# Conditioning columns of an encoder kernel, summed by VectorE from transposed weights

## The chip, the cores and the metric

The kernel runs on one core of a Trainium2 chip. The metric is the device time of one execution in microseconds, as the median of several runs; lower is better. Five engines work side by side, each through its own list of instructions in order: TensorE (PE; its weight loads are listed apart as PEld), VectorE (DVE), ScalarE (ACT), GpSimd (POOL) and SyncE (SP), which here issues nearly all transfers. They wait for one another by semaphores.

## The reference, cut to what matters

Two encoder layers over 512 tokens of width 1024, one with neighbourhood attention and one with Fourier mixing, each followed by a gated FFN. In every layer six vectors (shift, scale and gate of two sub-layers) come from one conditioning vector c:

```
cs = silu(c)                                     # 1024 values
mod = cs @ ada_w[i] + ada_b[i]                   # (1024) @ (1024 x 6144)
sh1, sc1, g1, sh2, sc2, g2 = split(mod, 6)
u = x * (1 + sc1) + sh1
x = layer_norm(ALPHA * x + (1 + g1) * mixer(u))
u = x * (1 + sc2) + sh2
x = layer_norm(ALPHA * x + (1 + g2) * conv_ffn(u))
```

All is float32. `ada_w` is 2 x 1024 x 6144, 50 MB, and is read once.

## The kernel before, in words

Activations lie transposed, features on the 128 partitions in eight chunks of 128 and tokens along the row. To keep float32 precision each operand is split into a rounded high half and the rest (`hi`, `lo`; `u0h`, `u0l`), and a product becomes three matmuls: high by high, high by low, low by high (`mm3`). ScalarE makes the high half (L232), VectorE the low one (L233).

A shift or a scale is needed as columns: feature k*128+p on partition p, column k. A gate is needed as a row. Both are summed in the same way: the weights come with the 1024 inputs on the partitions in eight tiles, VectorE scales each tile by its column of `cs` and adds it into an accumulator `acc` (L127, L129), and TensorE sums the accumulator over the partitions by a product with ones. This ends in one of three ways:

- First stage (`cond_first`, `cond_accumulate`, `cond_reduce`, `cond_finish`): for each chunk k of the input 256 columns of weights, shift and scale of that chunk, are accumulated (L400; the first steps on ScalarE, L398), reduced by four fp32 matmuls into the bank `red` (eight records in the trace), and finished by two small VectorE operations (L412, L413). Then ScalarE computes the input (L424, L425), VectorE its low half (L426), and TensorE runs 9 products of 512 columns for Q and K (`first_qk`) and 12 for V (`first_v`). Chunk 0 goes by `cond_first`, partly by fp32 matmuls of the raw weights with `cs`.
- `sum_cols`: for the FFN of layer 0, sixteen 1-column fp32 products (`sc`, `sh`), slipped between the triple products of the output projection `wo`.
- `ada_cols`: for the four other vectors of this kind, four 512-column products each with ones, and then VectorE takes the diagonal out of two banks. They stand in the up and down projections of the FFN of layer 0 (`steps_up0`, `steps_dn0`).

Tiles come from pools: `wraw` (4 buffers for raw weights), `big` (31 buffers of 4 KB a partition), `wsp`. A transfer is issued when its buffer is free, in the order of SyncE's list. GpSimd adds the attention bias tables (`bx`) and a mask, both loaded behind the first stage's weights, for the score maxima (L585), and scales the probabilities (L599). A scheduler orders each engine's list, except inside `tc.manual_schedule`, where it stays as written; `after` holds back what stands in it until an instruction is issued. The attention loop from its second pair on is already in written order.

Of the kernel before, what the change touches and what calls it, by code (L numbers as in the profile page):

```python
# [49 lines left out]

@with_exitstack
def tile_hybrid_encoder(ctx: ExitStack, tc: tile.TileContext, xT, x, cols_d, rows_d, ada0, ada_w, wqk0, wqk, wv,
# [5 lines left out]
    big = ctx.enter_context(tc.tile_pool(name="big", bufs=31))  # L58
# [24 lines left out]
    between = []  # L83

    def mm3(o, lh, ll, rh, rl, start, stop):
        mm(o, lh, rh, start, False)
        mm(o, lh, rl, False, False)
        mm(o, ll, rh, False, stop)
        if between:
            product, k = between.pop(0)  # L90
            product(k)
# [25 lines left out]


    def ada_accumulate(l, v, result):

        acc = None
        for k in range(KT):
            raw = wraw.tile([P, D], F32, tag="raw", name=f"ada_{l}_{v}_{k}")
            nc.sync.dma_start(out=raw, in_=ada_w[l, k * P : (k + 1) * P, v * D : (v + 1) * D])
# [24 lines left out]

    def ada_cols(accs, l, v, name):  # L150

        bs = ada_row_sums(accs[(l, v)], name)
        col = sml.tile([P, KT], F32, tag="adacol", name=f"{name}_col")
        for h in range(2):
            t = tmp.tile([P, 4, P], F32, tag="t", name=f"{name}_d{h}")
            V.tensor_tensor(out=t, in0=bs[h].rearrange("p (k q) -> p k q", q=P),
                            in1=ident.unsqueeze(1).to_broadcast([P, 4, P]), op=ALU.mult)
            V.tensor_reduce(out=col[:, 4 * h : 4 * h + 4], in_=t, axis=mybir.AxisListType.X, op=ALU.add)
        V.tensor_tensor(out=col, in0=col, in1=adab(l, v), op=ALU.add)
        return col  # L160

    def sum_cols(acc, name):

        b = bank(name)

        def product(k):
            mm(b[:, k : k + 1], acc[:, k * P : (k + 1) * P], f32(ones_r[:, 0:1]), True, True)

        between.extend((product, k) for k in range(KT))
        return b  # L170

    def biased(b, l, v, name):
        assert not between
        col = sml.tile([P, KT], F32, tag="adacol", name=f"{name}_col")
        V.tensor_tensor(out=col, in0=b[:, 0:KT], in1=adab(l, v), op=ALU.add)
        return col
# [174 lines left out]
    def load_chunk(k):  # L351

        raws = []
        n = 2 if k == 0 else 4
        for h in range(2):
            raw = bigt([P, 4, 256], F32, f"ada0_{k}_{h}")
            for i in range(0, 4, n):
                nc.sync.dma_start(out=raw[:, i : i + n, :], in_=ada0[k, :, 4 * h + i : 4 * h + i + n, :])
            raws.append(raw)
# [12 lines left out]
    accq, redq, done = {}, {}, {}  # L372

    def cond_first():

        acc, red = tmp.tile([P, 256], F32, tag="t", name="acc00"), bank("red", aux=True)
        for i in range(KT):
            r = raws[0][i // 4][:, i % 4, :]
            if i < 4:
                for b in range(2):  # L380
                    mm(red[:, b : b + 1], r[:, b * P : (b + 1) * P], cs[:, i : i + 1], i == 0 and b == 0, False)
            elif i == 4:
                V.tensor_scalar(out=acc, in0=r, scalar1=cs[:, i : i + 1], scalar2=None, op0=ALU.mult)
            else:
                V.scalar_tensor_tensor(out=acc, in0=r, scalar=cs[:, i : i + 1], in1=acc, op0=ALU.mult, op1=ALU.add)
        for b in range(2):
            mm(red[:, b : b + 1], acc[:, b * P : (b + 1) * P], f32(ones_r[:, 0:1]), False, b == 1)
        redq[0] = red

    def cond_accumulate(k):  # L390

        pair = tmp.tile([P, 2, 256], F32, tag="t", name="acc0")
        for i in range(KT):
            r, o = raws[k][i // 4][:, i % 4, :], pair[:, i % 2, :]
            if i < 2 and k == 1:
                V.tensor_scalar(out=o, in0=r, scalar1=cs[:, i : i + 1], scalar2=None, op0=ALU.mult)
            elif i < 2:
                A.mul(o, r, cs[:, i : i + 1])  # L398
            else:
                V.scalar_tensor_tensor(out=o, in0=r, scalar=cs[:, i : i + 1], in1=o, op0=ALU.mult, op1=ALU.add)  # L400
        accq[k] = pair

    def cond_reduce(k):
        pair, red = accq.pop(k), bank("red", aux=True)
        for b in range(2):
            for j in range(2):
                mm(red[:, b : b + 1], pair[:, j, b * P : (b + 1) * P], f32(ones_r[:, 0:1]), j == 0, j == 1)
        redq[k] = red

    def cond_finish(k):  # L410
        red = redq.pop(k)
        V.tensor_tensor(out=mod0[:, KT + k : KT + k + 1], in0=red[:, 0:1], in1=adab(0, 0)[:, k : k + 1], op=ALU.add)  # L412
        done["mod"] = V.scalar_tensor_tensor(out=mod0[:, k : k + 1], in0=red[:, 1:2], scalar=1.0,  # L413
                                             in1=adab(0, 1)[:, k : k + 1], op0=ALU.add, op1=ALU.add)
        x_ = xt[k // 2][:, k % 2, :]
        uh, ul = u0[0][k // 2][:, k % 2, :], u0[1][k // 2][:, k % 2, :]
        scale, bias = mod0[:, k : k + 1], mod0[:, KT + k : KT + k + 1]
        if k == 0:
            t = tmp.tile([P, S], F32, tag="t", name="u00")
            done["act"] = A.activation(out=uh, in_=x_, func=AF.Identity, scale=scale, bias=bias)  # L420
            V.tensor_scalar(out=t, in0=x_, scalar1=scale, scalar2=bias, op0=ALU.mult, op1=ALU.add)
            x_ = t
        else:
            A.activation(out=x_, in_=x_, func=AF.Identity, scale=scale, bias=bias)  # L424
            done["act"] = A.copy(out=uh, in_=x_)  # L425
        return V.tensor_tensor(out=ul, in0=x_, in1=f32(uh), op=ALU.subtract)  # L426
# [16 lines left out]
    cond_first()  # L443
    W.emit(iqk0[0])
    with after(cond_finish(0)):
        cond_accumulate(1)
    with after(done["act"]):
        W.emit(iv0[0])
    for k in range(KT):
        if k + 3 < KT:  # L450
            raws.append(load_chunk(k + 3))
        first_qk(k)
        if k + 1 < KT:
            cond_reduce(k + 1)
            cond_finish(k + 1)
        if k % 2 == 0 and k + 2 < KT:
            with after(done["act"]):
                W.emit(iv0[k // 2 + 1])
        if k + 2 < KT:
            with after(done["mod"]):  # L460
                cond_accumulate(k + 2)
        first_v(k)
# [189 lines left out]
    ada_list = [(0, 2), (0, 4), (0, 3), (0, 5), (1, 1), (1, 0), (1, 2), (1, 4), (1, 3), (1, 5)]  # L652

    def ada_iter():
        for l, v in ada_list:
            yield from ada_accumulate(l, v, accs)
# [173 lines left out]
    sc = sum_cols(accs[(0, 4)], "sc2_0")  # L830
    sh = sum_cols(accs[(0, 3)], "sh2_0")
# [4 lines left out]
    m1 = modulation(biased(sh, 0, 3, "sh2_0"), biased(sc, 0, 4, "sc2_0"), (0, 0), "ffn0")  # L836
# [15 lines left out]
    def steps_up0(f):  # L852
# [4 lines left out]
        if f == 12:  # L857
# [273 lines left out]
```

## Time and profile before

| | |
|---|---|
| median of 3 runs | 1066.25 us (1064.4 to 1066.55) |
| the profiled execution | 1064.35 us, span 1062.6 us |
| TensorE busy | 1045.4 us, 98% of the span |
| VectorE, ScalarE, GpSimd busy | 73%, 41%, 9% |
| transfers | 157.24 MB, mean 148 GB/s |

The span is the time from the first to the last instruction of the profiled execution. A matmul's record covers its latency, and records overlap: what a matmul costs is read from the distance of the starts, not from its duration.

### The profile page before, as it was taken

How to read it: one execution, taken by the hardware profiler on the slowest of the kernel's cores; microseconds unless marked ns; L12 is line 12 of the kernel's file. 1: busy time of each engine (PE TensorE's matmuls, PEld its weight loads, DVE VectorE, ACT ScalarE, POOL GpSimd, SP SyncE). 2: the span in 40 equal slices, each digit the busy share in tenths (PEclk: the TensorE clock that was granted, in tenths of full speed). 3: DMA queues.
4: the chain of work that ended last, by engine and by line, in shares of the span. 5: the costliest groups of instructions: out<-in, count | busy, mean ns of one | idle time of the engine just before them, and what ended most of it. 6: DMA issues, size and time to landing. Idle time of an engine off the chain costs nothing.

```text
span 1062.6 us, 13633 instructions
## 1 busy us (share of the span) xinstructions
PE 1045.4 (98%) x5140; PEld 875.8 (82%) x5140; DVE 771.0 (73%) x1227; ACT 433.6 (41%) x738; POOL 98.6 (9%) x136
## 2 busy tenths in 40 slices
PE   7999999999999999999999999999999999999996
PEld 6878888888988888888888788898888888888885
DVE  6779898867789888886654879868876666532366
ACT  4445566545544444444132135454344444422300
POOL 0133565600000000000000000000000000000000
PEclk9999999999999999999999999999999999999998
DMA  9877454550355756553885005313454333243301
GB/s 351 289 243 238 131 158 135 183 164 11 105 176 177 231 190 192 178 179 105 294 279 178 1 1 171 107 54 125 129 169 134 104 99 100 79 160 99 119 20 60
DMA packets 46290, 157.24 MB, mean 148 GB/s; under 512 B 5136, under 2 KB 7696, under 8 KB 46224
## 3 DMA queue, kind: packets, MB, share of 16 engines
q1 hardware_dynamic: 46080, 156.24, 44.3%
q8 instruction: 40, 0.66, 0.3%
q14 instruction: 26, 0.21, 0.1%
q10 hardware_dynamic: 144, 0.13, 0.0%
HBM read 154.25 MB, written 2.10 MB: 147 GB/s over the span
## 4 chain that ended last, share of the span: by engine, by line
PE 91%; DVE 3%; DMA 2%; POOL 2%; issue 1%; SPq 0%; ACT 0%; DVEq 0%; POOLq 0%; ACTq 0%
PE up L81 45%; PE dn L81 23%; PE wo L81 4%; PE qk L81 4%; PE fo L81 4%; PE v L81 2%; POOL p L599 1%; PE q L81 1%; PE av L634 1%; PE fy L81 1%; PE pt L620 1%; PE s L81 1%; PE tr L307 1%; PE red L81 1%; DMA bx<-in_rpb_dram 1%
## 5 line engine op out<-in xcount | busy, mean ns | idle before, releaser
L233 DVE TENSOR_TENSOR lo<-raw,hi 128x1024 fp32r<-128x1024 f32 (+1 forms) x173 | 209.8, 1221 | 126.4 <-ACT hi L232 125.9
L232 ACT CAST hi<-raw 128x1024 fp32r<-128x1024 f32 (+1 forms) x173 | 179.0, 1044 | 245.0 <-PE up L81 128.7
L81 PE MATMUL dn<-hi,h 128*128 128x512 f32 (+1 forms) x720 | 218.2, 384 | 0.0
L81 PEld LDWEIGHTS dn<-hi,h 128*128 128x128 f32 x720 | 134.2, 188 | 27.0
L81 PE MATMUL up<-u1l,hi 128*128 128x512 f32 (+1 forms) x384 | 142.7, 372 | 0.0
L81 PE MATMUL up<-u3h,hi 128*128 128x512 f32 (+1 forms) x384 | 142.8, 372 | 0.0
L81 PE MATMUL up<-u1h,lo 128*128 128x512 f32 (+1 forms) x384 | 142.7, 372 | 0.0
L81 PE MATMUL up<-u1h,hi 128*128 128x512 f32 (+1 forms) x384 | 142.6, 372 | 0.0
L81 PE MATMUL up<-u3l,hi 128*128 128x512 f32 (+1 forms) x384 | 142.6, 371 | 0.0
L81 PE MATMUL up<-u3h,lo 128*128 128x512 f32 (+1 forms) x384 | 142.6, 371 | 0.0
L81 PE MATMUL dn<-lo,h 128*128 128x512 f32 (+1 forms) x360 | 138.4, 384 | 0.0
L129 DVE SCALAR_TENSOR_TENSOR acc<-ada,cs,acc 128x1024 f32<-128x1024 f32 x70 | 92.4, 1321 | 11.3 <-DMA ada<-in_ada_w_dram 11.1
L267 POOL TENSOR_TENSOR y<-ve,mhalf 128x1 f32<-128x1 f32 x16 | 10.8, 672 | 833.6 <-DVE ve L265 833.6
L81 PEld LDWEIGHTS up<-u1l,hi 128*128 128x128 f32 x384 | 72.3, 188 | 12.6 <-DVE u1l L317 0.2
L81 PEld LDWEIGHTS up<-u3h,hi 128*128 128x128 f32 x384 | 72.3, 188 | 12.6
L81 PEld LDWEIGHTS up<-u1h,lo 128*128 128x128 f32 x384 | 72.3, 188 | 12.5
L81 PEld LDWEIGHTS up<-u1h,hi 128*128 128x128 f32 x384 | 72.2, 188 | 12.6
L81 PEld LDWEIGHTS up<-u3h,lo 128*128 128x128 f32 x384 | 72.3, 188 | 12.5
L81 PEld LDWEIGHTS up<-u3l,hi 128*128 128x128 f32 x384 | 72.3, 188 | 12.4
L81 PEld LDWEIGHTS dn<-lo,h 128*128 128x128 f32 x360 | 67.6, 188 | 13.5
L599 POOL TENSOR_SCALAR p<-p,rs 128x256 f32<-128x256 f32 x64 | 58.1, 926 | 63.7 <-DVE rs L597 63.5
L747 ACT ACTIVATE gel<-conv 128x512 f32<-128x512 f32 x44 | 27.8, 632 | 63.9 <-DVE conv L744 63.5
(220 smaller groups left out, 1600.8 us busy)
## 6 DMA issues: line engine op xcount, KB each, us to landing
raw<-in_up_dram SPq DMA_DIRECT2D x88, 512.0 KB, 3.6
ada<-in_ada_w_dram SPq DMA_DIRECT2D x80, 512.0 KB, 4.8
raw<-in_down_dram SPq DMA_DIRECT2D x44, 512.0 KB, 4.7
ada<-in_ada_dram SPq DMA_DIRECT2D x14, 512.0 KB, 10.8
raw<-in_wqk_dram SPq DMA_DIRECT2D x13, 512.0 KB, 5.0
raw<-in_wv_dram SPq DMA_DIRECT2D x8, 512.0 KB, 6.5
raw<-in_wo_dram SPq DMA_DIRECT2D x8, 512.0 KB, 3.5
raw<-in_fnwo_dram SPq DMA_DIRECT2D x8, 512.0 KB, 4.5
```

The source lines that it names most:

```text
L81: return T.matmul(o, lhsT=lhsT, rhs=rhs, start=start, stop=stop)
L129: V.scalar_tensor_tensor(out=acc, in0=raw, scalar=cs[:, k : k + 1], in1=acc, op0=ALU.mult, op1=ALU.add)
L232: A.copy(out=hi, in_=raw)
L233: eng.tensor_tensor(out=lo, in0=raw, in1=f32(hi), op=ALU.subtract)
L267: power = G.tensor_tensor(out=y, in0=ve, in1=mhalf, op=ALU.pow)
L307: T.transpose(out=b[:, j * P : (j + 1) * P], in_=X[s][:, k * P : (k + 1) * P], identity=ident)
L599: norm = G.tensor_scalar(out=pt[:, j, :], in0=pt[:, j, :], scalar1=rs[:, j : j + 1], scalar2=0.0, op0=ALU.mult, op1=ALU.add)
L620: T.transpose(out=o, in_=pt[:, j, f : f + P], identity=ident)
L634: T.matmul(b[:, o : o + e - a], lhsT=v, rhs=z[:, a:e][:, ::-1], start=n == 0 and m == 0, stop=n == 3 and m == 1, skip_group_check=True)
L747: A.activation(out=q, in_=t, func=AF.Square)
```

## The change

The weights of the shifts and scales lie transposed in memory: outputs on the partitions, inputs along the row. silu(c) is laid out once along a row and on all partitions (`cs_row`): eight fp32 matmuls of a `cs` column, broadcast, with the identity, into two banks, and two ScalarE copies. A VectorE instruction multiplies 1024 weights of a partition by `cs_row`, sums them, starts from the bias and writes one element of a column; its output goes over the raw weights. So eight such instructions make a whole column tile without TensorE. The gates stay as they were. The functions `cond_*`, `sum_cols`, `ada_cols` and `biased` go. The bytes and the order of the first stage's transfers stay. The first stage is written in issue order for VectorE, ScalarE and TensorE, and the pool `big` has 30 buffers.

```diff
-    big = ctx.enter_context(tc.tile_pool(name="big", bufs=31))
+    big = ctx.enter_context(tc.tile_pool(name="big", bufs=30))
...
+    cs_row = const.tile([P, D], F32, name="cs_row")
+
+    def fill_cs_row():
+        b = [bank(f"csb{h}", aux=True) for h in range(2)]
+        for k in range(KT):
+            mm(b[k // 4][:, k % 4 * P : (k % 4 + 1) * P], cs[:, k : k + 1].to_broadcast([P, P]), ident, True, True)
+        for h in range(2):
+            A.copy(out=cs_row[:, h * 512 : (h + 1) * 512], in_=b[h])
+
+
+    def weigh_rows(raw, c, col, start):
+
+        return V.tensor_tensor_reduce(out=raw, in0=raw, in1=cs_row[:, c], op0=ALU.mult, op1=ALU.add, scale=1.0,
+                                      scalar=start, accum_out=col)
+
+    def ada_columns(l, v, result):
+
+        for k in range(KT):
+            raw = wraw.tile([P, D], F32, tag="raw", name=f"ada_{l}_{v}_{k}")
+            nc.sync.dma_start(out=raw, in_=ada_w[ADA[(l, v)], k])
+            if k == 0:
+                col = const.tile([P, KT], F32, name=f"col_{l}_{v}")
+            weigh_rows(raw, slice(0, D), col[:, k : k + 1], adab(l, v)[:, k : k + 1])
+            if k == KT - 1:
+                result[(l, v)] = col
+            yield
...
+    def cond(k):
+
+        for b, start in enumerate((adab(0, 0), ada01)):
+            o = mod0[:, (1 - b) * KT + k : (1 - b) * KT + k + 1]
+            start = start[:, k : k + 1]
+            if k == 0:
+                half = sml.tile([P, 1], F32, tag="t0", name="half")
+                weigh_rows(raws[k][b][:, 0:512], slice(0, 512), half, start)
+                done["mod"] = weigh_rows(raws[k][b][:, 512:D], slice(512, D), o, half)
             else:
...
+                done["mod"] = weigh_rows(raws[k][b], slice(0, D), o, start)
...
-        for n, (w, u) in enumerate(((wh, uh), (wh, ul), (wl, uh))):
+        for n, (w, u) in enumerate(((wh, uh), (wl, uh), (wh, ul))):
...
+    with tc.manual_schedule(engines={mybir.EngineType.DVE, mybir.EngineType.Activation, mybir.EngineType.PE}):
+        fill_cs_row()
+        cond(0)
+        first_input(0)
         W.emit(iv0[0])
...
+        cond(1)
+        for k in range(KT):
+            if k + 3 < KT:
+                raws.append(load_chunk(k + 3))
+            first_qk(k)
+            W.emit(iv0[k // 2] if k % 2 == 0 else iqk0[k // 2 + 1] if k + 1 < KT else iqk[1][1])
+            if k + 1 < KT:
+                first_input(k + 1)
+            if k + 2 < KT:
+                cond(k + 2)
+            first_v(k)
...
-    sc = sum_cols(accs[(0, 4)], "sc2_0")
-    sh = sum_cols(accs[(0, 3)], "sh2_0")
...
-    m1 = modulation(biased(sh, 0, 3, "sh2_0"), biased(sc, 0, 4, "sc2_0"), (0, 0), "ffn0")
+    m1 = modulation(accs[(0, 3)], accs[(0, 4)], (0, 0), "ffn0")
...
-        if f == 12:
-            fst["sc"] = ada_cols(accs, 1, 1, "sc1_1")
...
-            m = modulation(ada_cols(accs, 1, 0, "sh1_1"), fst["sc"], (0, 1), "fn")
+            m = modulation(accs[(1, 0)], accs[(1, 1)], (0, 1), "fn")
...
-        if f == 4:
-            fst["sc"] = ada_cols(accs, 1, 4, "sc2_1")
         if f == 8:
-            fst["m3"] = modulation(ada_cols(accs, 1, 3, "sh2_1"), fst["sc"], (1, 0), "ffn1")
+            fst["m3"] = modulation(accs[(1, 3)], accs[(1, 4)], (1, 0), "ffn1")
```

On TensorE the program begins so before, up to the first product with the low weights (`q`, `k`: banks of the first two heads; `u0h`, `u0l`: the halves of the input's first chunk pair):

```order
L81 MATMUL red<-cs,ada_0_0_112 128x1 x8
L81 MATMUL red<-ones_r,acc_139 128x1 x2
L81 MATMUL q_109<-u0h_96,hi_155 128x512
L81 MATMUL k_110<-u0h_96,hi_155 128x512
L81 MATMUL q_111<-u0h_96,hi_155 128x512
```

and so after the change:

```order
L84 MATMUL csb_144<-ident,cs 128x128 x4
L84 MATMUL csb_145<-ident,cs 128x128 x4
L84 MATMUL q_110<-u0h_97,hi_164 128x512
L84 MATMUL k_111<-u0h_97,hi_164 128x512
L84 MATMUL q_112<-u0h_97,hi_164 128x512
```

The products with the raw weights make room for the eight that lay out silu(c), which need no weights.

Between the Q and K products of a chunk and its V products (`v_0` to `v_3`: four token blocks), in the middle of the first stage, TensorE has this before:

```order
L81 MATMUL q_109<-u0h_98,lo_304 128x512
L81 MATMUL k_110<-u0h_98,lo_304 128x512
L81 MATMUL q_111<-u0h_98,lo_304 128x512
L81 MATMUL red<-ones_r,acc_413 128x1 x4
L81 MATMUL v_0_105<-hi_307,u0h_98 128x512
L81 MATMUL v_1_106<-hi_307,u0h_98 128x512
```

and this after:

```order
L84 MATMUL q_110<-u0l_103,hi_299 128x512
L84 MATMUL k_111<-u0l_103,hi_299 128x512
L84 MATMUL q_112<-u0l_103,hi_299 128x512
L84 MATMUL v_0_106<-hi_333,u0h_99 128x512
L84 MATMUL v_1_107<-hi_333,u0h_99 128x512
```

The four `red` matmuls are gone, and the products with the low input stand last instead of in the middle.

VectorE has, for one to two chunks of the first stage, before:

```order
L400 SCALAR_TENSOR_TENSOR acc_259<-ada_3_0_178,cs,acc_259 128x256 x2
L400 SCALAR_TENSOR_TENSOR acc_259<-ada_3_1_180,cs,acc_259 128x256 x4
L426 TENSOR_TENSOR u0l_101<-xt_133,u0h_97 128x512
L412 TENSOR_TENSOR mod_104<-red,cols 128x1
L413 SCALAR_TENSOR_TENSOR mod_104<-red,cols 128x1
L400 SCALAR_TENSOR_TENSOR acc_311<-ada_4_0_230,cs,acc_311 128x256 x2
L400 SCALAR_TENSOR_TENSOR acc_311<-ada_4_1_232,cs,acc_311 128x256 x2
```

and after (the rows named ISA are the sums, with the read of the accumulator behind each):

```order
L397 TENSOR_TENSOR u0l_102<-xt_136,u0h_98 128x512
L128 ISA ada_3_0_176,mod_105<-ada_3_0_176,cs_row,cols 128x1024
L128 ISA mod_105 128x1
L128 ISA ada_3_1_178,mod_105<-ada_3_1_178,cs_row,ada_113 128x1024
L128 ISA mod_105 128x1
L229 TENSOR_TENSOR lo_260<-raw_140,hi_259 128x1024
L397 TENSOR_TENSOR u0l_102<-xt_136,u0h_98 128x512
```

The small operations behind `red` are gone, two sums of 1024 elements stand in place of six accumulations of 256, and the split of the next weights stands where VectorE waits for ScalarE's input.

## Rows read from the trace of the kernel before

**Rows 1.** The page: busy time of the engines; the chain's shares by engine.

```profile
PE 1045.4 (98%) x5140; PEld 875.8 (82%) x5140; DVE 771.0 (73%) x1227; ACT 433.6 (41%) x738; POOL 98.6 (9%) x136
...
PE 91%; DVE 3%; DMA 2%; POOL 2%; issue 1%; SPq 0%; ACT 0%; DVEq 0%; POOLq 0%; ACTq 0%
```

**Rows 2.** By stretch: PE, PEld, DVE, ACT, POOL busy, clock, DMA share, GB/s.

```profile
0.00:40.00 40.00, 32.75 (x151) 27.26 (x151) 25.76 (x61) 17.52 (x27) 0.87 (x8) 1.00 0.96 366
40.00:60.00 20.00, 19.75 (x96) 16.08 (x95) 15.14 (x29) 11.45 (x17) 4.14 (x6) 1.00 0.56 171
```

**Rows 3.** Timeline to 17 us: start, duration, engine, what [idle before, releaser].

```profile
3.79 0.17 DVE L116 TENSOR_TENSOR cs<-cs,cols 128x8 f32<-128x8 f32 x1
...
4.96 3.49 PEld L81 LDWEIGHTS red<-cs,ada 128*128 128x128 f32 x16 [4.96 <-DVE cs L116]
...
9.18 0.83 ACT L232 CAST hi<-raw 128x768 fp32r<-128x768 f32 x1 [5.86 <-DMA raw<-in_wqk_dram]
...
10.34 0.81 ACT L420 ACTIVATE u0h<-xt,mod 128x512 fp32r<-128x512 f32 x1 [0.33 <-DVE mod L413]
...
11.21 0.79 PE L81 MATMUL q<-u0h,hi 128*128 128x512 f32 x1 [1.16 <-ACT u0h L420]
...
14.36 0.63 PE L81 MATMUL k<-u0h,lo 128*128 128x512 f32 x1
...
14.79 0.63 PE L81 MATMUL q<-u0h,lo 128*128 128x512 f32 x1
...
16.38 1.18 PE L81 MATMUL v<-hi,u0h 128*128 128x512 f32 x4
```

**Rows 4.** Timeline of one chunk of the first stage, 39 to 47 us.

```profile
39.52 0.95 PE L81 MATMUL red<-ones_r,acc 128*128 128x1 f32 x8
...
40.33 1.17 PE L81 MATMUL v<-hi,u0h 128*128 128x512 f32 x4
...
40.58 0.15 DVE L413 SCALAR_TENSOR_TENSOR mod<-red,cols 128x1 f32<-128x1 f32 x1
...
42.27 0.69 DVE L426 TENSOR_TENSOR u0l<-xt,u0h 128x512 fp32r<-128x512 f32 x1
...
46.09 1.17 PE L81 MATMUL v<-hi,u0h 128*128 128x512 f32 x4
```

**Rows 5.** Timeline: a wait of TensorE, and the end of the first stage.

```profile
25.79 0.38 PE L81 MATMUL red<-ones_r,acc 128*128 128x1 f32 x2 [0.56 <-DVE acc L400]
...
59.14 1.07 PE L81 MATMUL v<-lo,u0h 128*128 128x512 f32 x4
```

**Rows 6.** Groups by line and shape: busy us, mean ns of one, idle before.

```profile
L233 DVE TENSOR_TENSOR lo<-raw,hi 128x1024 fp32r<-128x1024 f32 x169 | 205.9, 1227 | 126.4 <-ACT hi L232 125.9
...
L129 DVE SCALAR_TENSOR_TENSOR acc<-ada,cs,acc 128x1024 f32<-128x1024 f32 x70 | 92.4, 1321 | 11.3 <-DMA ada<-in_ada_w_dram 11.1
...
L754 DVE TENSOR_TENSOR h<-conv,h 128x512 fp32r<-128x512 f32 x44 | 30.3, 688 | 11.0 <-ACT h L753 11.0
...
L476 ACT CAST v<-v 128x512 fp32r<-128x512 f32 x8 | 4.2, 590 | 0.0
```

**Rows 7.** Timeline of VectorE in the score maxima of the first heads.

```profile
64.64 0.42 DVE L585 CUSTOM_DVE_ANT_0 p<-s,bm 128x256 f32<-128x256 f32 x1
...
64.99 0.42 DVE L585 CUSTOM_DVE_ANT_0 p<-s,bm 128x256 f32<-128x256 f32 x1
```

**Rows 8.** Timeline of TensorE in the wo stage.

```profile
202.24 0.48 PE L81 MATMUL wo<-hi,ao 128*128 128x512 f32 x1
...
203.02 0.28 PE L81 MATMUL sc<-ones_r,acc 128*128 128x1 f32 x2
203.16 0.48 PE L81 MATMUL wo<-hi,ao 128*128 128x512 f32 x1
```

**Rows 9.** Timeline of TensorE in the up projection of layer 0.

```profile
397.97 0.39 PE L81 MATMUL sc<-sc_hi,ones_r 128*128 128x512 f32 x1
...
398.90 0.40 PE L81 MATMUL up<-u1h,hi 128*128 128x512 f32 x1
```

**Rows 10.** The chain that ended last, two pieces: start, duration, what.

```profile
76.19 5.76 DMA ada<-in_ada_w_dram
...
84.67 5.34 DMA raw<-in_wqk_dram
```

**Rows 11.** VectorE alone by stretch: busy us, clock, DMA share, GB/s.

```profile
100.00:200.00 100.00, 88.52 (x205) 1.00 0.45 143
```

More of the change, by code (lines that the diff above doesn't have):

```diff
@@ L48 @@
 ROW_LNB = 8
+ADA = {lv: i for i, lv in enumerate([(0, 2), (0, 4), (0, 3), (0, 5), (1, 1), (1, 0), (1, 2), (1, 4), (1, 3), (1, 5)])}
 @with_exitstack
@@ L87, in mm3 @@
         mm(o, lh, rl, False, False)
[L88 to L91, printed above, removed]
+        return mm(o, ll, rh, False, stop)
     cols = const.tile([P, NCOLS], F32, name="cols")
@@ L123, in ada_accumulate @@
             raw = wraw.tile([P, D], F32, tag="raw", name=f"ada_{l}_{v}_{k}")
-            nc.sync.dma_start(out=raw, in_=ada_w[l, k * P : (k + 1) * P, v * D : (v + 1) * D])
+            nc.sync.dma_start(out=raw, in_=ada_w[ADA[(l, v)], k])
             if k == 0:
@@ L148, in ada_row_sums @@
         return res
[L150 to L176, printed above, removed]
     def bcast_row(r, name):
@@ L353, in load_chunk @@
         raws = []
[L354 to L358, printed above, removed]
+        for b in range(2):
+            raw = bigt([P, D], F32, f"ada0_{k}_{b}")
+            for h in range(2 if k == 0 else 1):
+                c = slice(h * 512, (h + 1) * 512) if k == 0 else slice(0, D)
+                nc.sync.dma_start(out=raw[:, c], in_=ada0[k, :, b, c])
             raws.append(raw)
@@ L370, in load_chunk @@
         return raws
[L372 to L383, printed above, removed]
-            else:
[L385 to L414, printed above, removed]
+    done = {}
@@ L419, in cond_finish @@
             t = tmp.tile([P, S], F32, tag="t", name="u00")
-            done["act"] = A.activation(out=uh, in_=x_, func=AF.Identity, scale=scale, bias=bias)
             V.tensor_scalar(out=t, in0=x_, scalar1=scale, scalar2=bias, op0=ALU.mult, op1=ALU.add)
+            W.emit(iqk0[0])
+            A.activation(out=uh, in_=x_, func=AF.Identity, scale=scale, bias=bias)
             x_ = t
@@ L424, in cond_finish @@
             A.activation(out=x_, in_=x_, func=AF.Identity, scale=scale, bias=bias)
-            done["act"] = A.copy(out=uh, in_=x_)
-        return V.tensor_tensor(out=ul, in0=x_, in1=f32(uh), op=ALU.subtract)
+            A.copy(out=uh, in_=x_)
+        V.tensor_tensor(out=ul, in0=x_, in1=f32(uh), op=ALU.subtract)
     def first_qk(k):
@@ L650, in evict_values @@
         ao[p] = t
-    ada_list = [(0, 2), (0, 4), (0, 3), (0, 5), (1, 1), (1, 0), (1, 2), (1, 4), (1, 3), (1, 5)]
     def ada_iter():
-        for l, v in ada_list:
-            yield from ada_accumulate(l, v, accs)
+        for l, v in ADA:
+            yield from (ada_accumulate if v in (2, 5) else ada_columns)(l, v, accs)
     ada = ada_iter()
@@ L1068, in _layouts, with piece @@
         + [f[f"ln{i}_b"][l] for l in range(DEPTH) for i in (1, 2)]))
-    a0 = f["ada_w"][0].reshape(KT, P, 6, KT, P)[:, :, 0:2]
-    r["ada0"] = np.ascontiguousarray(a0.transpose(3, 1, 0, 2, 4).reshape(KT, P, KT, 2 * P))
-    r["ada_w"] = f["ada_w"]
+    def piece(l, v):
+        w = f["ada_w"][l][:, v * D : (v + 1) * D]
+        return (w if v in (2, 5) else w.T).reshape(KT, P, D)
+    r["ada0"] = np.ascontiguousarray(np.stack([piece(0, 0), piece(0, 1)], axis=2))
+    r["ada_w"] = np.ascontiguousarray(np.stack([piece(l, v) for l, v in ADA]))
     wq = f["na_w_qkv"][0]
```

23 lines of the change are left out of this document (3 added, 20 removed).

## Prediction

> **What bounds the kernel now.** I read the page first: TensorE is busy for 98% of the span and holds 91% of the chain that ended last [rows 1]. So in most of the span a matmul that goes away is time that goes away, and work of VectorE, ScalarE or the queues counts only where TensorE waits for it. The exception to look at is the start, so the second view was the busy time of the first 40 us: the 16 DMA engines are 96% busy at 366 GB/s and TensorE has 32.75 of 40 us [rows 2]. Third, the timeline of that stage. The sigmoid product `cs` is there at 3.96 us, and the first product of the network starts at 11.21 [rows 3]. Its first products lie 0.43 us apart (14.36 to 14.79), those from 16.4 on about half of that. [...]
>
> From 30 us on the stage runs in a fixed beat of 5.76 us a chunk (40.33 to 46.09), of which the eight records of the `red` matmuls take 0.81 (39.52 to 40.33) [rows 4]. The other 4.95 are 21 products at 0.235. Before 30 us TensorE also waited for sums of VectorE, as at 25.79 [rows 5]. The stage's last four products start at 59.14, so it ends at about 60.2 [rows 5].
>
> **The change part by part.** All sums go against the profiled execution, 1064.35 us; the median of the three runs, 1066.25, lies 1.9 above it, and the forecast is for such a median.
>
> *Head of the first stage.* New: eight fp32 matmuls lay silu(c) along the rows of two PSUM banks, ScalarE copies the banks, and VectorE then sums four half rows one after the other. fp32 matmuls of 128 columns at this clock are in no row. The nearest are the 16 records of `red<-cs,ada`, 3.49 us or 0.22 each, where loading weights sets the pace [rows 3]; eight new matmuls should be 16 records too. If streaming 128 columns doesn't hide behind the loading, a record costs up to 0.43, what a 512-column product takes there. I take 0.22, since loading and streaming overlap in all neighbouring rows. Then bank 0 is full at 3.96+0.1+1.75 = 5.8, bank 1 at 7.6. The nearest copy out of PSUM is the V eviction, 590 ns [rows 6]: row halves at 6.5 and 8.3. Nothing in the trace waits for the weights that long.
>
> The sum of a row is the same kind of instruction as the score maxima, a custom VectorE operation with an accumulator read behind it, which comes every 0.35 us at 256 elements [rows 7]. Per element I take the slope between 512 and 1024 elements of plain fp32 operations, (1227-688)/512 = 1.05 ns [rows 6]. That makes 0.61 us for 512 and 1.15 for 1024. The ends: 1.15 if the accumulator costs nothing per element, 2.2 if adding halves the rate. I take 1.15: the maxima fit that slope, 256 x 1.05 = 0.27 and 0.08 over, with their accumulator.
>
> So the four halves end at 6.5+0.6 = 7.1, then 8.3+3x0.61 = 10.15; ScalarE's pass over the input takes 0.81 more [rows 3], and the first product starts at about 11.1 against 11.21. The 8 old `red` products and the accumulations are gone and the start is the same: no gain there. Weights of Q and K are there at 9.18 [rows 3], no hindrance. Edit at nothing: the new order (high, low weights, then low input) is the same nine products.
>
> *The beat.* Chunk 0: nine products at 0.43 = 3.9, twelve at 0.235 = 2.85, end at 17.9. Seven more at 4.95 end at 52.6, against 60.2: **-7.6 us**. Of that 7 x 0.81 = 5.7 is the `red` matmuls, the rest the waits before 30 us. It holds only if VectorE keeps up. Its loop for a chunk: from the end of the modulation (40.73) through ScalarE's two passes to the end of the low half (42.96) 2.23 us [rows 4], plus two sums, 2.3, plus handing over 0.1: 4.6, under 4.95. The split of the next weights (1.23) fits in the 1.5 in which VectorE waits for ScalarE. With 1.32 a sum, what an accumulation of 1024 elements takes [rows 6], the loop is level with the beat and still nothing is lost; this is the narrow place. Transfers: the order and bytes of the queue are unchanged, and what must land up to the last chunk's rows (sixteen row tiles of 0.52 MB, four inputs of 0.52, four pairs of weights of 0.92, the columns: 14.3 MB) is in at 366 GB/s by 39 us [rows 2]; its product isn't due before 47.6, its sums before 43.4. In SyncE's list the next pair's key weights, which wait for a free buffer, now stand ahead of the bias tables; the mask stood behind them before as well, and GpSimd needs both, so nothing new is late.
>
> *wo stage.* Sixteen 1-column products leave the matmul sequence, two records each. Three products and one of them take 0.92 us (202.24 to 203.16) [rows 8]; three products alone, at 0.93/4 of [rows 9], 0.70. That is 0.22 each, **-3.6 us**. The columns are ready earlier, so nothing waits in their place.
>
> *Both FFNs.* Four times four 512-column products leave: 0.93 us each time (397.97 to 398.90) [rows 9], **-3.7 us**. The copies, subtractions and reductions with them were covered by TensorE and bring nothing. In exchange 48 sums of 1024 elements replace 42 accumulations of 1321 ns and six cheaper first steps [rows 6]; 1.15 to 1.32 against these is no more work, under TensorE's cover (one `big` buffer less, six accumulators fewer).
>
> *What follows the first stage.* From 60 to 97 the chain runs through transfers and VectorE, as 5.76 us for `ada` and 5.34 for `wqk` [rows 10]. These are released by the softmax and by freed buffers, so I let them move along with the stage's end.
>
> Sum: 1064.35 - 7.6 - 3.6 - 3.7 = 1049.45; as a median, +1.9, **1051.3 us**.
>
> **Rivals.**
>
> *B, a later head.* At 0.43 a record bank 1 is full at 11.0, the first product at 14.5: +3.4. Or TensorE, which now has nothing between 7.6 and 11.1, stays at the slow spacing for the twelve V products of chunk 0 as well: 12 x 0.195 = +2.3. For it: before, `red` products stood in that gap. Against: the first nine were slow before too. 1053.5 to 1057. [...]
>
> *C, the gain of the first stage is lost to transfers*, inside it (96% busy) or behind it, where the chain is made of landings [rows 10] that would not come 7.6 us earlier. For it: those landings are in the chain. Against: from 40 to 60 us the DMA engines are 56% busy [rows 2], so there is room to come earlier. All lost: 1058.9; half: 1055.
>
> *D, slower: the sum of 1024 elements runs at half rate, 2.2 us.* Then VectorE sets the beat in the first stage: 2.23+4.4+0.1 = 6.7 a chunk in place of 4.95, less where its slack of the first chunks carries over. Worked through chunk by chunk the stage ends at about 66, +5.8. In the attention stage VectorE has 11.5 us of 100 left [rows 11], and 14 sums at +0.9 are 12.3, so up to 12 come on top; -7.3 is still saved. 1066.25+5.8-7.3+(0 to 12): around 1071 if the attention stage pays most. It decides from about 1.95 us a sum. Against: the maxima, with the same accumulator, run at the slope of plain operations [rows 6, 7]. [...]
>
> *That the change doesn't do what it says* would be C: the matmuls go, and something else takes their time.
>
> **How the numbers follow.** Forecast A (all three terms, within 2.5 us) 0.66; B 0.16; C 0.13; D 0.05. Likeliest 1051.3, its own range 1048.5 to 1054. For 8 in 10 the range must reach into B and C: 1048 to 1058. What a measurement of this kernel can tell from no change is about 0.2%, 2.1 us: A, B and C are all faster by more; of D some ends near no change. Faster 0.95, same 0.01, slower 0.04.
>
> **What would show it.** Right: no `red`, `sc` or `sh` products; the first product at 11 to 11.5; V to V 4.95 us a chunk; the last V products near 52; the custom operation at 1.15 to 1.25 us; wo and FFN shorter by 3.6 and 3.7. Wrong: a first product after 12.5 (B, see the `csb` records and the slow spacing); TensorE waiting for VectorE's modulation in the beat, with sums over 1.4 (D); or waits for `wqk`, `ada` or bias landings between 50 and 95 (C). The prediction falls if the time between the end of the first stage and the start of the wo stage grows by more than 2 us, since I let all of it move along.

## The result and the profile after

After the change the median is **1051.05 us** (1050.14 to 1051.14, 4 runs) against 1066.4 of the kernel before in the same session; the ratio is 0.9853, with a 95% interval of 0.9832 to 0.9874. That is 15 us off. The profiled execution took 1050.14 us, its span is 1048.1 us, against 1064.35 and 1062.6 before.

The page of after, busy time and the chain that ended last, against [rows 1]:

```profile
PE 1029.5 (98%) x5032; PEld 862.9 (82%) x5032; DVE 759.5 (72%) x1218; ACT 425.2 (41%) x720; POOL 102.6 (10%) x136
...
PE 88%; DVE 5%; POOL 2%; DMA 2%; ACT 1%; issue 1%; SPq 0%; DVEq 0%; POOLq 0%; ACTq 0%
```

TensorE's busy time fell by 15.9 us, a little more than the span (14.5). VectorE has less to do, not more (759.5 against 771.0), but its share of the chain rose from 3% to 5%.

The timeline of after, in the order of the program: head, two chunks of the first stage, its end, and the last pair of heads in the wo stage.

```profile
4.16 3.48 PEld L84 LDWEIGHTS csb<-ident,cs 128*128 128x128 f32 x16 [4.16 <-issue]
...
6.27 0.58 ACT L123 COPY cs_row<-csb 128x512 f32<-128x512 f32 x1 [2.87 <-PE csb L84]
6.88 0.75 DVE L128 CUSTOM_DVE_ANT_0 ada<-ada,cs_row,cols 128x512 f32<-128x512 f32 x1 [2.84 <-ACT cs_row L123]
...
8.59 0.75 DVE L128 CUSTOM_DVE_ANT_0 ada<-ada,cs_row,half 128x512 f32<-128x512 f32 x1 [0.95 <-ACT cs_row L123]
...
10.06 0.75 DVE L128 CUSTOM_DVE_ANT_0 ada<-ada,cs_row,half 128x512 f32<-128x512 f32 x1
...
10.85 0.81 ACT L392 ACTIVATE u0h<-xt,mod 128x512 fp32r<-128x512 f32 x1 [0.88 <-DVE mod L128]
...
11.72 0.80 PE L84 MATMUL q<-u0h,hi 128*128 128x512 f32 x1 [3.78 <-ACT u0h L392]
...
14.87 0.63 PE L84 MATMUL k<-u0l,hi 128*128 128x512 f32 x1
...
15.30 0.51 PE L84 MATMUL q<-u0l,hi 128*128 128x512 f32 x1
...
22.59 0.69 DVE L397 TENSOR_TENSOR u0l<-xt,u0h 128x512 fp32r<-128x512 f32 x1 [0.67 <-ACT u0h L396]
23.20 1.28 DVE L128 CUSTOM_DVE_ANT_0 ada<-ada,cs_row,cols 128x1024 f32<-128x1024 f32 x1
...
23.27 0.40 PE L84 MATMUL q<-u0h,hi 128*128 128x512 f32 x1
...
24.40 1.28 DVE L128 CUSTOM_DVE_ANT_0 ada<-ada,cs_row,ada 128x1024 f32<-128x1024 f32 x1
...
28.12 0.40 PE L84 MATMUL q<-u0h,hi 128*128 128x512 f32 x1
...
51.48 1.07 PE L84 MATMUL v<-lo,u0h 128*128 128x512 f32 x4
...
197.48 7.52 POOL L566 TENSOR_SCALAR p<-p,rs 128x256 f32<-128x256 f32 x8 [8.31 <-DVE rs L564]
...
201.74 0.38 PE L587 MATMUL pt<-ident,p 128*128 128x128 f32 x2
...
202.78 2.82 PE L587 MATMUL pt<-ident,p 128*128 128x128 f32 x14 [0.66 <-POOL p L566]
```

Four things are to be seen. The layout of silu(c) takes 16 records of 0.22 us, and the first product starts at 11.72, half a microsecond later than before [rows 3]. A chunk now takes 4.85 us (23.27 to 28.12) instead of 5.76 [rows 4]. The last four V products start at 51.48 instead of 59.14 [rows 5]. And in the wo stage TensorE comes to the last pair's transposes while GpSimd still scales the probabilities: after two transposes it waits 0.66 us, and the sixteen spread over almost 4 us.

The sums by shape (busy us, mean ns, idle before):

```profile
L128 DVE CUSTOM_DVE_ANT_0 ada<-ada,cs_row,cols 128x1024 f32<-128x1024 f32 x55 | 72.6, 1330 | 11.7 <-DMA ada<-in_ada_w_dram 11.7
L128 DVE CUSTOM_DVE_ANT_0 ada<-ada,cs_row,ada 128x1024 f32<-128x1024 f32 x7 | 9.0, 1282 | 0.0
```

A record is 1.28 us long; back to back the sums are 1.20 to 1.21 us apart (23.20 to 24.40).

Where the time went shows best between marks that both programs pass. Starts in us, from the two timelines on TensorE (scores: the first product of pair 0; `fs`: the first product of the Fourier sub-layer):

| mark | before | after | between marks, after less before |
|---|---|---|---|
| first product | 11.21 | 11.72 | +0.51 |
| first scores | 60.13 | 52.48 | -8.16 (first stage) |
| first `wo` | 198.69 | 190.84 | -0.20 (attention) |
| first `up` | 252.12 | 242.01 | -2.26 (wo stage) |
| first `dn` | 497.86 | 485.79 | -1.96 (up projection) |
| first `fs` | 620.99 | 606.62 | -2.30 (down projection) |
| last product | 1053.93 | 1039.45 | -0.11 |

### The profile page after: what moved, and what is told of

Same layout as the page of the kernel before. It is cut to its first block, busy times and chain, and to the rows that moved or that the text cites. A ratio compares the mean times of both kernels' runs of the same rounds, so it can differ in the third digit from the quotient of the medians.

```text
span 1048.1 us, 13339 instructions
## 1 busy us (share of the span) xinstructions
PE 1029.5 (98%) x5032; PEld 862.9 (82%) x5032; DVE 759.5 (72%) x1218; ACT 425.2 (41%) x720; POOL 102.6 (10%) x136
## 4 chain that ended last, share of the span: by engine, by line
PE 88%; DVE 5%; POOL 2%; DMA 2%; ACT 1%; issue 1%; SPq 0%; DVEq 0%; POOLq 0%; ACTq 0%
PE up L84 44%; PE dn L84 23%; PE qk L84 4%; PE fo L84 4%; PE wo L84 3%; POOL p L566 2%; PE v L84 2%; PE q L84 1%; PE fy L84 1%; PE av L601 1%; DVE p L552 1%; DMA ada<-in_ada_w_dram 1%; PE pt L587 1%; PE s L84 1%; DVE ada L128 1%
## 5 line engine op out<-in xcount | busy, mean ns | idle before, releaser
L128 DVE CUSTOM_DVE_ANT_0 ada<-ada,cs_row,cols 128x1024 f32<-128x1024 f32 (+1 forms) x56 | 73.4, 1320 | 14.6 <-DMA ada<-in_ada_w_dram 11.7
```

Of the source, the lines that this page charges most:

```text
L128: return V.tensor_tensor_reduce(out=raw, in0=raw, in1=cs_row[:, c], op0=ALU.mult, op1=ALU.add, scale=1.0, scalar=start, accum_out=col)
```

## The experiments

The theory to test: every term is time of matmuls that TensorE no longer runs, what follows moves along, and the differences from the forecast are waits that the removed matmuls used to cover. The main rivals: the gain comes from the written order, or transfers and VectorE set the pace. Times are medians, ratios are to the kernel before in the same session, and "earlier" or "later" is read from the traces at the marks above, against after. Differences of 1 to 2 us between variants lie within the intervals; for these only the marks speak. But there is one trace for each kernel: three with the same first stage (after, the shared scalings, the other wo order) have their first scores at 52.48, 52.93 and 53.15, so a difference of under 0.7 us there says nothing.

**The first stage alone.** Everything behind the first stage is as before.

```diff
-            yield from (ada_accumulate if v in (2, 5) else ada_columns)(l, v, accs)
+            yield from ada_accumulate(l, v, accs)
...
+        if f == 12:
+            fst["sc"] = ada_cols(accs, 1, 1, "sc1_1")
```

> The first stage as after the change, everything later as before it: plain weights, accumulators, and the matmuls of the wo stage and of both FFN projections. Theory A (every term is matmul time off TensorE, and what follows the first stage moves along): the last V products start near 51.5 us, and the whole is 7.2 to 7.8 us shorter than before, near 1058.9. Rival C (the earlier end is lost again to landings between 50 and 95 us): under 4 us. The wo stage then reaches its last pair with the full sixteen small products between its triples, so the wait for GpSimd should be absent.

Measured: 1057.42 us, ratio 0.9924 (0.9909 to 0.9939). The first scores start at 52.54, 7.6 us earlier than before; first `wo` 8.3, last product 8.2 earlier. Nothing is lost on the way, so rival C falls. The wo stage takes 53.69 us, with the sixteen small products, against 53.43 before, and no wait for GpSimd is among its waits.

**The late part alone.** The first stage is as before; silu(c) is laid out behind the projections of pair 1.

```diff
     QK[1] = q, evict_k(1, proj_qk(1)[1])
+    fill_cs_row()
```

> The first stage as before, everything later as after; the row of silu(c) is laid out behind the projections of the second pair instead of at the start. Eight fp32 matmuls of 128 columns at the faster spacing cost 0.9 to 1.8 us of TensorE there. Theory A: wo 2.6 to 3.6, the two FFN projections 3.7 to 4.0, less 0.9 to 1.8: 4.5 to 6.7 us shorter than before, near 1060.5. If the two parts interact (VectorE has no room in the attention stage for sums when the first stage is late), less than 4.

Measured: 1061.85 us, ratio 0.9964 (0.9950 to 0.9978). That is 3.8 us by the ratio and 2.85 between the medians, under the expected 4.5 to 6.7 and in the range of the rival, less than 4. The profiled execution, 1059.32, is the fastest of five (the others took 1061.7 to 1062.4), and its marks give 5.0; what the others lost no trace shows. By the marks the parts are where they should be: wo stage -2.24, up -1.96, down -2.35, and attention +1.93, which is the layout:

```profile
68.27 1.05 PE L84 MATMUL csb<-ident,cs 128*128 128x128 f32 x8
...
72.59 1.05 PE L84 MATMUL csb<-ident,cs 128*128 128x128 f32 x8
```

Sixteen records at the faster spacing, 2 x 8 x 0.12 = 1.9 us. Without the layout the two parts give 8.2 + 5.0 + 1.9 = 15.1 us at the last product, and after gives 14.5: they add but for 0.6. (By the ratios it is 8.1 + 3.8 + 1.9 = 13.8 against 15.7, within the intervals.) The wait for GpSimd (0.7 us) is here too, though the wo stage begins 1.6 us later than in before. So it isn't due to an earlier start, but to the sixteen products that are gone.

**The order by the scheduler.** After, with the first stage not written out.

```diff
-    with tc.manual_schedule(engines={mybir.EngineType.DVE, mybir.EngineType.Activation, mybir.EngineType.PE}):
+    if True:
```

> As after, but the first stage is ordered by the scheduler and not as written; the matmuls are gone in both. In its order VectorE and ScalarE split the first two weight tiles ahead of the sums of chunk 0, and the sums of chunk 1 stand between those of chunk 0. If the written order matters only at the head (theory A, which put the gain of the beat down to the matmuls), the first product comes 2 to 5 us later than 11.7, the beat stays at 4.85, and the whole is 2 to 5 us over after. Rival: the order makes the beat, then chunks take over 5.2 us and it is over 5 us slower than after.

Measured: 1055.19 us, ratio 0.9904 (0.9888 to 0.9921). The beat is the same: from the first product to the first scores 40.63 us, in after 40.76. All of the loss is at the head:

```profile
9.52 0.83 ACT L228 CAST hi<-raw 128x768 fp32r<-128x768 f32 x1 [6.23 <-DMA raw<-in_wqk_dram]
...
11.77 1.06 ACT L123 COPY cs_row<-csb 128x512 f32<-128x512 f32 x2
11.90 1.23 DVE L229 TENSOR_TENSOR lo<-raw,hi 128x1024 fp32r<-128x1024 f32 x1 [0.56 <-ACT hi L228]
...
13.04 0.75 DVE L128 CUSTOM_DVE_ANT_0 ada<-ada,cs_row,cols 128x512 f32<-128x512 f32 x1
...
16.71 0.79 PE L84 MATMUL q<-u0h,hi 128*128 128x512 f32 x1 [8.89 <-ACT u0h L392]
```

The splits stand ahead of the copies and of the sums, and both engines wait for weights that land at 9.5 us with the copies queued behind. The written order is worth 5 us here; it adds nothing to the gain of the beat.

**The four matmuls put back.**

```diff
             first_qk(k)
+            if k + 1 < KT:
+                red = bank("red", aux=True)
+                for b in range(2):
+                    for j in range(2):
+                        mm(red[:, b : b + 1], cs_row[:, (2 * j + b) * P : (2 * j + b + 1) * P],
+                           f32(ones_r[:, 0:1]), j == 0, j == 1)
```

> As after, with four fp32 matmuls of one column (eight records) put back into each of the first seven chunks, between the products for Q and K and those for V; they read the row of silu(c) and nobody reads them, so no wait comes with them. Theory A (TensorE sets the beat): 0.81 a chunk, beat 5.66, +5.7 us over after, near 1056.7. Rival (VectorE's loop or the transfers set the beat of 4.85, and the old matmuls were beside them): +0 to +2.

Measured: 1056.66 us, ratio 0.9923 (0.9906 to 0.9941); the profiled execution was the slowest of four, 1059.32.

```profile
15.41 1.70 PE L84 MATMUL red<-ones_r,cs_row 128*128 128x1 f32 x8
16.97 2.05 PE L84 MATMUL v<-hi,u0h 128*128 128x512 f32 x4
18.83 1.91 PE L84 MATMUL v<-hi,u0l 128*128 128x512 f32 x4
...
23.79 0.95 PE L84 MATMUL red<-ones_r,cs_row 128*128 128x1 f32 x8
24.60 1.17 PE L84 MATMUL v<-hi,u0h 128*128 128x512 f32 x4
25.61 1.08 PE L84 MATMUL v<-hi,u0l 128*128 128x512 f32 x4
...
29.55 0.95 PE L84 MATMUL red<-ones_r,cs_row 128*128 128x1 f32 x8
```

From 23.79 to 29.55 the beat is 5.76 us, exactly that of before, with VectorE's work and the transfers of after. So the matmuls made the beat. They cost 5.76-4.85 = 0.91 a chunk: 0.81 up to the next product and 0.1 more behind it, since the four V products after them take 1.01 (24.60 to 25.61) and not 0.92. Seven times 0.91 is 6.4 us of the 8.16 between the first product and the first scores. The other 1.8 lie in three chunks of before, which took 8.00, 6.82 and 6.27 us (from 11.21, 19.21 and 48.92 on), two of them with waits of TensorE (0.56 us at 25.79 [rows 5], 0.24 at 50.03); no run put these back. The first chunk shows another thing: the products stay at the slow spacing until about 20.5 us (the four from 18.83 on are 0.43 apart), where after has the faster one from 15.65 (0.23 apart). From the first product to the second chunk's first it is 10.26 us and in after 6.69, so beside the 0.91 some 2.7 us are the spacing. The granted clock of that stretch is about half:

```profile
12.00:22.00 10.00, 10.00 (x31) 8.17 (x30) 8.07 (x12) 3.75 (x6) 0.00 (x0) 0.55 1.03 410
```

**A third sum for every chunk.**

```diff
                 done["mod"] = weigh_rows(raws[k][b], slice(0, D), o, start)
+                if b == 1:
+                    idle = sml.tile([P, 1], F32, tag="t0", name="idle")
+                    weigh_rows(raws[k][b], slice(0, D), idle, start)
```

The column `idle` is not used, so the output is the same.

> As after, but in chunks 1 to 7 of the first stage VectorE makes a third sum of 1024 elements, a repeat of the second (over the products that the second left in its tile) into a column that nobody reads. VectorE's loop becomes 4.64+1.21 = 5.85 us against a beat of 4.85. Theory A's narrow place: from some chunk on TensorE waits for the low half, the beat goes to 5.85, and the stage ends 3 to 7 us later. This is also what rival D would have looked like with sums of about 1.8 us. If VectorE has more slack than its loop shows, +0 to 2.

Measured: 1053.63 us, ratio 0.9885 (0.9872 to 0.9899); the first scores are 3.9 us later, of which 0.6 are already there at the start of the second chunk, by the spacing. TensorE now waits for the low half of the V weights in two chunks:

```profile
28.41 1.20 PE L84 MATMUL v<-lo,u0h 128*128 128x512 f32 x4 [0.46 <-DVE lo L229]
39.10 1.19 PE L84 MATMUL v<-lo,u0h 128*128 128x512 f32 x4 [0.70 <-DVE lo L229]
```

These chunks take 5.60 and 5.83 us. A third one, from 44.99 on, takes 6.43; there TensorE waits 0.69 us for a high half from ScalarE, and VectorE's third sum has a record of 1.63 us and not 1.28. VectorE's loop became 5.35 us on average and not 5.85, because its waits for ScalarE (0.40 and 0.67 in turn) vanished in it. So in after VectorE works 4.1 of the 4.85 us: 2 x 1.21 for the sums, 1.68 for the rest. It would be level with TensorE at (4.85-1.68)/2 = 1.58 us a sum, an estimate from these rows; the narrow place was wider than the 1.32 of the prediction.

**Head: bank 0 first.** Both sums of chunk 0 that need the first bank stand ahead of those that need the second.

```diff
+        half = [sml.tile([P, 1], F32, tag=f"t{b}", name=f"half{b}") for b in range(2)] if k == 0 else None
+        for b, start in enumerate((adab(0, 0), ada01)):
+            if k == 0:
+                weigh_rows(raws[k][b][:, 0:512], slice(0, 512), half[b], start[:, 0:1])
...
-                weigh_rows(raws[k][b][:, 0:512], slice(0, 512), half, start)
-                done["mod"] = weigh_rows(raws[k][b][:, 512:D], slice(512, D), o, half)
+                done["mod"] = weigh_rows(raws[k][b][:, 512:D], slice(512, D), o, half[b])
```

> As after, but in chunk 0 VectorE first sums the two half rows that need bank 0 and then the two that need bank 1. In after the second sum waits for the copy of bank 1 (it starts at 8.59), and two more follow it. Here only two follow the copy: first product 0.7 to 0.8 us earlier, near 11.0, whole -0.7. If the input or its weights end last instead, 0.

Measured: 1049.77 us, ratio 0.9846 (0.9832 to 0.9859). The first product is 0.64 earlier, the first scores 0.83, the last product 1.0.

```profile
11.08 0.50 PE L84 MATMUL q<-u0h,hi 128*128 128x512 f32 x1 [3.21 <-ACT u0h L394]
11.42 0.40 PE L84 MATMUL k<-u0h,hi 128*128 128x512 f32 x1
11.65 0.40 PE L84 MATMUL q<-u0h,hi 128*128 128x512 f32 x1
11.89 0.53 PE L84 MATMUL q<-u0h,lo 128*128 128x512 f32 x1
12.22 0.63 PE L84 MATMUL k<-u0h,lo 128*128 128x512 f32 x1
```

The place was right: TensorE is idle for 3.21 us ahead of the first product, and for 3.78 or 3.79 in after and in the five other runs with its head and order. Unexpected: the first products are 0.23 apart and those from 12.22 on 0.43. The faster spacing was there and was lost again.

**TensorE kept busy at the head.**

```diff
             A.copy(out=cs_row[:, h * 512 : (h + 1) * 512], in_=b[h])
+        for n in range(8):
+            mm(vb[n // 4][:, n % 4 * P : (n % 4 + 1) * P], ident, ident, True, True)
```

> As after, with eight fp32 matmuls of the identity by itself put on TensorE behind the layout of silu(c), into banks that the V products start afresh later. They fill the time from 7.9 to about 11.4 us in which TensorE is idle in after. Theory of the head: the slow spacing (0.43 us for 512 columns) of the first nine products ends a fixed time after the first product whatever stands before, so nothing changes: 0 to +0.3. Rival: what TensorE does before decides when the spacing falls; then some of the nine products run at 0.235 from the start, -0.5 to -1.8 us.

Measured: 1049.6 us, ratio 0.9846 (0.9832 to 0.9859).

```profile
7.71 3.01 PE L84 MATMUL v<-ident 128*128 128x128 f32 x16
11.70 0.50 PE L84 MATMUL q<-u0h,hi 128*128 128x512 f32 x1 [0.98 <-ACT u0h L394]
12.04 0.40 PE L84 MATMUL k<-u0h,hi 128*128 128x512 f32 x1
...
17.95 0.51 PE L84 MATMUL q<-u0h,hi 128*128 128x512 f32 x1 [1.13 <-ACT u0h L398]
```

My theory of the head falls: with TensorE busy up to 0.98 us ahead of them all nine products run at the faster spacing (0.23 to 0.34), so here what stands before made the difference. They end 1.7 us earlier, and the next wait takes it: chunk 1's input is late by 1.13 us, and the first scores are only 0.2 us earlier, which is within the spread.

**The scalings shared**, for the last pair only.

```diff
-            norm = G.tensor_scalar(out=pt[:, j, :], in0=pt[:, j, :], scalar1=rs[:, j : j + 1], scalar2=0.0,
+            norm = (V if p == PAIRS - 1 and j > 1 else G).tensor_scalar(out=pt[:, j, :], in0=pt[:, j, :], scalar1=rs[:, j : j + 1], scalar2=0.0,
```

> As after, but of the eight scalings of the last pair's probabilities VectorE does four (two of each head) and GpSimd the other four. In after they end last ahead of the transposes, one in 0.94 us on GpSimd, and the wo stage is only 2.3 us shorter than before where 3.6 were forecast. Theory: TensorE's waits for them in the wo stage (about 1.3 us) go, and so does 1.0 to 1.3 us of the time. If the missing gain lies elsewhere, 0.

**The wo stage in another order.**

```diff
-    transpose_probs(PAIRS - 1)
     wo_part(2, first, True, False, (0,))
+    transpose_probs(PAIRS - 1)
...
-    vbanks = weigh_values(PAIRS - 1)
     wo_part(2, first, True, False, (1,))
+    vbanks = weigh_values(PAIRS - 1)
```

> As after, but in the wo stage the twelve products of the third tile's first half stand ahead of the last pair's transposes, and those of its second half ahead of the weighing of values; GpSimd scales all eight as in after. The wait for GpSimd (0.66 and more) is covered by 2.8 us of products. Sharing the scalings between engines only moved the wait to VectorE's copies of the transposes (1.22 us). Theory: the missing 1.3 us of the wo stage are these two waits; both covered, the stage from the first wo product to the first up product goes from 51.17 to 49.9. Rival: PSUM banks, of which there are six, are short in either order, and TensorE waits for a bank instead: 0 to -0.4.

Measured: 1049.66 us, ratio 0.9845 (0.9832 to 0.9859), for the first, 1049.45, ratio 0.9857 (0.9842 to 0.9872), for the second. The wo stage takes 50.73 and 50.54 us, in after 51.17. In both the wait for GpSimd is gone and another stands in its place. TensorE's waits, of the shared scalings and then of the other order (us in total, times, longest):

```profile
PE wo L84 <- DVE ptl L444: 1.2, 1, 1.2
```

```profile
PE wo L84 <- DVE ao L616: 0.8, 1, 0.8
```

In the first TensorE waits for VectorE's low halves of the transposes, in the second for the last pair's output. So the missing 1.3 us seem to lie in the chain of the last pair (scaling, transposes, copies, weighing, copies), where each move uncovers the next link; 0.44 and 0.63 of them came back. Both moves together were not tried, so that the rest lies there too is not shown.

**Sums straight out of PSUM**, on top of the new order of the halves, and then with five identity matmuls and chunk 1's sums ahead of a subtraction.

```diff
-        return V.tensor_tensor_reduce(out=raw, in0=raw, in1=cs_row[:, c], op0=ALU.mult, op1=ALU.add, scale=1.0,
+        return V.tensor_tensor_reduce(out=raw, in0=raw, in1=cs_row[:, c] if by is None else by, op0=ALU.mult, op1=ALU.add, scale=1.0,
```

> As head_order, and the four half sums of chunk 0 read silu(c) from the PSUM banks instead of waiting for ScalarE's copies (the later sums use the copies). Bank 0 is full at about 6.1, bank 1 at 7.9; sums of 0.7 us each end at 9.3 and the first product starts near 10.2, against 11.08 in head_order and 11.72 in after: 0.8 to 0.9 us off head_order. If reading both operands, one of them from PSUM, makes a sum slower (over 1 us a half), the gain is gone.

```diff
-        W.emit(iv0[0])
         cond(1)
+        W.emit(iv0[0])
```

> As head_psum, with five identity matmuls behind the layout of silu(c) on TensorE (some 2 us, to end before the first product), and chunk 1's two sums ahead of the subtraction for the first V weights in VectorE's list. Alone the identity matmuls brought the nine first products to 0.235 us apart, and the gain was lost to a wait of 1.13 us for chunk 1's input. Theory: that wait was VectorE's list; with chunk 1's sums 1.2 us earlier the nine products at the faster spacing show in the time: first stage ends 2.5 to 3.5 us earlier than in after. If chunk 1's rows land too late for it, or a new wait for the low V weights comes, 1 to 1.5.

Measured: 1048.81 us, ratio 0.9853 (0.9839 to 0.9868), for the first, 1050.11, ratio 0.9863 (0.9846 to 0.9879), for the second. The first, on the timeline:

```profile
6.81 0.75 DVE L129 CUSTOM_DVE_ANT_0 ada<-ada,csb,cols 128x512 f32<-128x512 f32 x1 [2.85 <-ACT cs_row L123]
...
9.27 0.83 ACT L229 CAST hi<-raw 128x768 fp32r<-128x768 f32 x1 [1.10 <-DMA raw<-in_wqk_dram]
...
10.01 0.81 ACT L395 ACTIVATE u0h<-xt,mod 128x512 fp32r<-128x512 f32 x1
10.87 0.80 PE L84 MATMUL q<-u0h,hi 128*128 128x512 f32 x1 [3.33 <-ACT u0h L395]
```

A sum that reads PSUM is as fast (0.75 us), but it starts at 6.81, behind ScalarE's copy and not with it; and then ScalarE, which must first split weights that land at 9.27, is late. The first product is 0.21 us earlier than in the order alone, not 0.8, and the sums did not do it: this split starts at 9.27 here and at 9.47 in the order alone. In all four runs with the new order the first product follows the start of the split by 1.60 to 1.61 us (it starts at 9.71 and 9.64 in the other two). The second shows what is next:

```profile
7.70 1.28 PE L84 MATMUL v<-ident 128*128 128x128 f32 x10
...
9.71 0.83 ACT L231 CAST hi<-raw 128x768 fp32r<-128x768 f32 x1 [1.23 <-DMA raw<-in_wqk_dram]
...
11.31 0.79 PE L84 MATMUL q<-u0h,hi 128*128 128x512 f32 x1 [2.33 <-ACT u0h L397]
11.91 0.63 PE L84 MATMUL k<-u0h,hi 128*128 128x512 f32 x1
...
12.96 1.28 DVE L131 CUSTOM_DVE_ANT_0 ada<-ada,cs_row,cols 128x1024 f32<-128x1024 f32 x1 [0.82 <-DMA ada<-in_ada_dram]
```

Ten records in 1.28 us, the faster level, then 2.33 us without work, and the products are back at 0.43. Chunk 1's sum waits for its rows, which land at 12.96. Both expectations fail. The landing of the first weights now sets the first product, and that of chunk 1's rows is the next bound. (The first scores are 0.6 us earlier here; the last product is 1.6 us later, since attention lost 2.2 us in this execution, where the granted clock is 0.85 from 90 to 100 us.)

**The moves together.** The last two, `head_all` and `wo_order`, with no further edit.

> head_all and wo_order together. If their gains are apart in time and TensorE is the bound between, they add: 3.5 to 4.5 us off after by the theories, 1 to 2 by the rivals.

Measured: 1048.84 us, ratio 0.9852 (0.9837 to 0.9867); first scores 0.7, last product 0.85 us earlier than in after. The gains don't add up to more than one of them. The sums out of PSUM have the earliest last product, 1.7 us ahead of after, and the lowest median, 1048.81; but their ratio is that of after, and part of the 1.7 is the landing of the weights and the spacing in that one execution. Which variant is best stays open.

## Why the prediction was right

It said 1051.3, and 1051.05 came. The mechanism held: matmuls that leave TensorE take their time with them, and what follows moves along. That the number came so close is in part luck. The three terms gave 14.2 us in the profiled execution (1064.35 to 1050.14) where 14.9 were forecast, and the median of after lies 0.9 above that execution where the forecast added 1.9. By its own steps:

- **Head, forecast no gain, first product at 11.1.** It came at 11.72, 0.5 later than before (at 11.34 to 11.74 in five other traces with this head, and at 10.81 in the other trace with the old one). The 16 records of 0.22 were right. Mis-sized: the halves. The copies end 0.3 later (8.55), and the three sums behind the second take 2.22 us and not 1.83, because a sum of 512 takes 0.68 and hands its result to the next one 0.1 later.
- **The sum, forecast 1.15 for 1024 and 0.61 for 512.** It measures 1.21 and 0.68. The slope of 1.05 ns an element held ((1.21-0.68)/512 = 1.04); what is fixed is 0.14 and not 0.08. Rival D, half the rate, is out.
- **The beat, forecast 4.95, of it the matmuls 0.81.** It is 4.85, and the matmuls cost 0.91. The stage's last products start 7.66 us earlier, where 7.6 was forecast: a later head and a shorter beat cancel. The forecast put what the matmuls don't explain down to waits before 30 us; a part of it, 0.5 us, lay in the chunk from 48.92 on.
- **What follows moves along.** From the first scores to the first `wo` it is 138.36 us, before it was 138.56: it holds. Of rival C there is nothing.
- **wo stage, forecast -3.6.** It gave -2.26, and here a step failed: "nothing waits in their place". The forecast considered only the columns. The sixteen products had also covered GpSimd's scalings, and TensorE now waits for them.
- **Both FFN projections, forecast -3.7.** They gave -4.26. The up projection gave 1.96 for 1.86. In the down projection the eight products had stood in ones and twos among others, and the stretch gave 2.30 for 1.86; where the kind changes, the trace of before has five steps of 0.31 to 0.34 us there and not 0.23 (as from 586.27 to 586.61 and to 586.92).

With the head's half microsecond inside the first stage, the terms give 7.65 + 0.20 + 2.26 + 4.26 + 0.11 = 14.5, where 14.9 were forecast. The errors of +1.3 (wo) and -0.6 (FFN) partly cancelled; the closeness of the total owes something to that.

**Rival B** did not show in the trace of after, but what it describes was seen in others. With five identity matmuls the layout's sixteen records took 0.22 us each and the ten behind it 1.28 us in all; then TensorE was idle for 2.33 us, and the products behind stood 0.43 to 0.60 apart at a granted clock of 0.63 (from 10 to 14 us). With eight it was idle for 0.98 us, and they stood 0.23 to 0.34 apart at 1.00. What exactly sets the spacing these traces leave open: with the new order of the halves three products ran fast after 3.21 us idle before them. The slow start of the first nine products cost nothing against before, because before paid the same for its own. That it ended with them in after is luck of the execution: in the third sum, which has the same head, the granted clock is 0.59 from 14 to 18 us, the slow spacing reaches into the V products as B said, and chunk 0 takes 7.65 us and not 6.69, 0.96 of the 2.3 that B gave it.

## What to carry to other kernels

A matmul with one column of output was not a small one here: sixteen records with one column took 3.49 us at the start of before [rows 3], sixteen with 128 columns 3.48 in after. Put four such matmuls back, and the beat is what it was, 0.91 us longer. When such fillers leave a sequence, look at what else they covered, not only at what they fed: the chain of another engine that ended just in time will now be waited for. And a sum on an engine with slack is free only until the slack is gone, so read that engine's work without its waits, not its loop.

## What was unexpected of the hardware

- TensorE's spacing can rise and fall within a few microseconds. In the run with the bank order the first products were 0.23 us apart, those half a microsecond later 0.43, and from 15.77 on they were at the fast level again.
- The moment at which the spacing falls to 0.23 for good differs between executions with the same products at the head. Chunk 0 takes 6.69 us in after, and 6.93, 7.16, 7.34 and 7.65 in four others (the first stage alone, the shared scalings, the other wo order, the third sum). This may be what spreads single runs of one kernel over 1 to 3 us; with one trace for each kernel it stays an argument.
- A granted clock of 1.00 at the start can mean that there is no record. From 10 to 14 us the row has 0.59 in the run with the matmuls put back and 0.75 in that with the bank order, but 1.00 in after and before, with the same 0.43 us between products. In the traces of the last two the first record of the clock is its rise, at 15.55 and 15.78 us, and a stretch without a record is shown as 1.00; where there are records, they agree with the spacing. So the spacing is what to go by at the start.
- A product-and-sum of VectorE that reads PSUM takes 0.75 us for 512 elements in the run with the sums out of PSUM, the same as from SBUF in after (0.75).
